# First weights through two kinds of raw tiles, two cache copies placed late, and one buffer pair of decode's keys given to raw weights and evictions

## The chip, the cores and the metric

The program runs on one core of a Trainium2 chip (trn2). The metric is the device time of one execution in microseconds (us). Before the change it was 1180.13 us, the median of 3 runs (1179.48 to 1180.59). Lower is better.

## What is computed

Two layers of a streaming encoder, for a prompt of 1024 tokens and, in the same launch, for 8 sequences that each get 16 new tokens on top of cached keys and values of 1024 tokens. The width is 1024, everything is float32. Cut to what matters:

```python
# layer 0 (A): differential attention + attention to a memory of 256 tokens
q, k, v, gd, mq, gm = a_project(x, w_in_a, cos, sin)          # prompt and samples
od = diff_finish(diff_attend(q, k or cache + k, v or cache + v, mask, lam), g, lam_init)
om = mem_attend(mq, mk, mv)                                   # samples: cached mk, mv
x  = layer_norm(alpha * x + concat(od * silu(gd), om * silu(gm)) @ w_out, ln_g, ln_b)
# layer 1 (B): one shared K/V from x, sliding window of 128 with sinks + memory attention
sks = concat([cache_swa_k, skn], axis=1); svs = concat([cache_swa_v, svn], axis=1)
...                                                           # the same merge
swa_ks, swa_vs = sks[:, -128:], svs[:, -128:]                 # updated rolling buffer
```

The last line is where the two DRAM-to-DRAM copies of this case come from: rows 16 to 127 of the old window caches are an output, copied as they are.

## The kernel before

The tokens are 9 tiles of 128 rows: tiles 0 to 7 are the prompt, tile 8 holds the 128 new tokens. The inputs stand transposed in SBUF as a high and a low part (`th`, `tl`), each weight tile of 128x512 likewise (`wh`, `wl`): float32 is split into two parts, and a product is three products of parts, high by high, high by low and low by high. So each raw tile that is loaded is cast by ScalarE into the high part (line 110) and subtracted from it by VectorE or GpSimd into the low part (line 113). After that the raw tile is free.

Raw tiles come in kinds, with so many buffers each (`RAWS`, line 39): `wraw` for weights, `draw` for decode's cached keys and values and some other inputs of the new tokens, `ev` for what is evicted from the projections' banks on its way to DRAM, and for the x rows of the output projection. The split parts of weights have 8 buffers (`wh`, `wl`), those of decode's raw tiles 4 (`dkh`, `dkl`, function `dk_tiles`). A kind named in `RING` takes its buffers in turn; all `load`s are issued by SyncE (line 119).

`run` puts the weights of all projections into one plan in the order in which they are needed. It first loads the eight weight tiles of the keys and values of heads 0 and 1 (`kvA`, 0; tensor `wA`) with eight calls of `preload(1)`; these subtract on GpSimd and VectorE in turn. Then come `load_x`, which loads each x tile in two halves through buffers called `kh` and `P0` (tile 8 first), and `setup` with small constants. The first projection (`project_kv`) runs the 9 tiles through the eight weights: 24 products of 128x512 a tile, into one of two banks `pj` (line 184). Next is the projection of the queries (`project_q`, weights `wQT`, products of 128x384). Then layer A runs attention of the prompt, decode of the cached sequences (`diff_dec_s` and `diff_dec_v`, whose keys and values go through `raw_split`, `draw` and `dk_tiles`) and the other projections as background. At its end `layer_end` projects the new tokens (`out_first` for tile 8). The two copies `swko` and `swvo` are emitted right after that, in `run`, lines 1407 and 1408.

The order in which instructions are emitted is not the order in which they run. The class `Order` collects all instructions, works out who depends on whom (`depend`: overlapping regions of tiles and tensors, from line 1481), gives each a duration by a table of its own (`cost`), and makes a list schedule over the five engines and the DMA rings (`schedule`), four passes with due times fed back (`due`). An instruction that writes a tile first has to wait there for a free buffer of that kind, and the buffers of a kind are given in the order of emission (`place`). The best of the four orders is then fixed on each engine (`keep`). An instruction that depends on nothing and holds no tile may stand anywhere in it. SyncE runs its issues in that fixed order, one at a time, and waits at an issue whose buffer isn't free.

Of the kernel before, what the change touches and what calls it, by code (L numbers as in the profile page):

```python
# [12 lines left out]
F32R = mybir.dt.float32r  # L13
# [22 lines left out]
HEADS = [1, 2]  # L36
URGENT = 4000
RING = ("wh", "wl", "dkh", "dkl", "draw", "P0", "dP", "ldk")
RAWS = {"wraw": 3, "draw": 4, "ev": 2}
RATES = {('A', 0): (1.0, 3.5, 4), ('A', 1): (0.8, 1.76, 4), ('m', 0): (1.6, 3.25, 7), ('B', 0): (2.17, 2.16, 5), ('B', 1): (0.9, 3.0, 4), ('m', 1): (1.32, 2.18, 5)}  # L40
DECODE = 1.76
DECODE_FIRST = (8, 0, 1, 2, 3, 4, 5, 6, 7)
# [22 lines left out]
class Kernel:  # L65
# [49 lines left out]
    def load(self, tag, src):  # L115
        raw = self.t2([128, 512], tag, bufs=RAWS[tag])[:, :math.prod(src.shape[1:])]
        if len(src.shape) == 3:
# [127 lines left out]
    def setup(self):  # L245
# [14 lines left out]
        nc.gpsimd.memset(self.nhalf, -0.5)  # L260
        lv = self.t2([128, 4, 64], "ev", bufs=RAWS["ev"])
        nc.sync.dma_start(lv, d["lam"].rearrange("o a b -> (o a b)").partition_broadcast(128).rearrange("p (a b) -> p a b", b=64))
        lp = self.t2([128, 2, 64], "ev", bufs=RAWS["ev"])
        nc.vector.tensor_tensor(lp, lv[:, 0::2, :], lv[:, 1::2, :], op=ALU.mult)
# [49 lines left out]
        per = 512 // src.shape[2]  # L314
        self.plan += [(key, src[:, k:k + per, :]) for k in range(0, src.shape[1], per)]

    def preload(self, n, el="dve"):

        for key, src in self.plan[:n]:
            h, lo = (self.take(self.wpool, [128, 512], F32R, x, 8) for x in ("wh", "wl"))  # L320
            c = src.shape[2]
            view = lambda x: x.rearrange("p (a b) -> p a b", b=c)
            self.load_split(view(h), view(lo), "wraw", src, "act", el)
            w = self.loaded.setdefault(key, ([], []))
            for x, y in ((h, w[0]), (lo, w[1])):
                y += [x[:, j * c:(j + 1) * c] for j in range(src.shape[1])]
        del self.plan[:n]
# [310 lines left out]
        self.nc.vector.tensor_tensor_reduce(out, o, x, -1.0, TOP, ALU.add, ALU.min, nm)  # L638

    def dk_tiles(self, n=512):  # L640
        return [self.t2([128, 512], x, F32R, bufs=4)[:, :n] for x in ("dkh", "dkl")]

    def p_tile(self, dt=F32):
        return self.t2([128, 512], "dP", dt, bufs=3)
# [714 lines left out]
    def run(self):  # L1359
        d = self.d  # L1360
        src = {("kvB", 0): d["wKV"]}
        for j in range(4):
            src["gs", j] = d["wBT"][j]
        for l in range(2):
            src["kvA", l], src["gA", l] = d["wA"][l], d["wGA"][l]
            for i in range(2):
                src["M", l, i], src["O", l, i] = d["wM"][l, i], d["wO"][l, i]
            for j in range(4):
                src["q", l, j] = d["wQT"][l, j]
                for i, x in enumerate("qg"):  # L1370
                    src[f"m{x}{l}", j] = (d["wBT"][4:12] if l else d["wAT"])[2 * j + i]
        plan = []
        for l in range(2):
            plan += [("kvB", 0) if l else ("kvA", 0)] + [("q", l, j) for j in range(4)] + ORDER[l] + [("O", l, g) for g in range(2)]
        plan = [(key, src[key]) for key in plan]
        for key, src in plan:
            if key[0] == "M":
                for k in range(0, NK, 2):
                    self.planned(("MT", *key[1:], k), d["memT"][:, k:k + 2, :])
                    self.planned((*key, k), src[:, k:k + 2, :])  # L1380
            else:
                self.planned(key, src)
        for k in range(NK):
            self.preload(1, ("pool", "dve")[k % 2])
        self.load_x()
        self.setup()
        self.background(("kvA", 0), self.layer_a_kv(0))
        self.background(("q", 0), self.project_q(0, (2, 0, 1)))
        for key in ORDER[0]:
            self.background(key, self.filler(*key))  # L1390
        self.finish(("kvA", 0))
        units = [self.diff_dec_units(0), self.diff_dec_units(1), self.mem_dec_units(0)]
        dec = self.side(self.weave(*[[u for g in units for u in g[i]] for i in range(2)]))
        self.layer_a(dec)

        def store(dst, z):
            for c in range(2):
                cols = slice(c * 512, (c + 1) * 512)
                self.nc.sync.dma_start(dst[:, cols], z[:, cols])

        def turn(t, z):
            store(self.x1[t], z)
            self.to_T(t, z[:, 0:512], z[:, 512:1024])

        self.background(("O", 0, 1), self.out_second(0, turn))
        d = self.d
        self.nc.sync.dma_start(d["swko"], d["csk_n"][:, 16:128, :])
        self.nc.sync.dma_start(d["swvo"], d["csv_n"][:, 16:128, :])
        self.background(("kvB", 0), self.layer_b_kv())
        self.finish()  # L1410
        self.background(("q", 1), self.project_q(1, (0, 1, 2)))
        for key in ORDER[1]:
            self.background(key, self.filler(*key))
        self.phase(("B", 0))
        self.credit, self.rate = 0.0, 8.0
        K, V = self.layer_b_build()
        self.need((("q", 1), 0))
        units = [self.swa_dec_units(), self.mem_dec_units(1)]
        dec = self.side(self.weave(*[[u for g in units for u in g[i]] for i in range(2)]))
        self.layer_b(K, V, dec)  # L1420
        self.background(("O", 1, 1), self.out_second(1, lambda t, z: store(d["y"][t], z)))
        self.finish()
# [3 lines left out]
class Order:  # L1426
# [53 lines left out]

    def depend(self):

        self.seen, past = {}, collections.defaultdict(list)
        self.pred, self.uses = [], []
        for i, ins in enumerate(self.ins):
            pred, names = set(), set()
            ops = [(w, self.regions(a)) for w, x in ((0, ins.ins), (1, ins.outs)) for a in x if hasattr(a, "bass_ap")]
            for w, (name, p, m) in ops:
                names.add(name)
                bank = name in self.tiles and self.tiles[name][2]  # L1490
                pred.update(j for j, w2, p2, m2 in past[name] if j != i and p & p2 and m & m2
                            and (w or w2 or bank and self.engine[j] != self.engine[i]))
                past[name].append((i, w, p, m))
            for w, (name, p, m) in ops:
                if w:
                    past[name] = [x for x in past[name] if x[0] == i or x[2] & ~p or x[3] & ~m]
            self.pred.append(pred)
            self.uses.append([x for x in names if x in self.tiles])
        self.succ = [[] for _ in self.ins]
        for i, pred in enumerate(self.pred):  # L1500
            for j in pred:
                self.succ[j].append(i)
# [313 lines left out]
```

## Time and profile before

| | |
|---|---|
| median of 3 runs | 1180.13 us (1179.48 to 1180.59) |
| the profiled execution | 1177.22 us, span 1175.4 us |
| TensorE busy, products | 1120.6 us (95%), 6404 |
| VectorE busy | 823.9 us (70%) |
| ScalarE busy | 731.1 us (62%) |
| GpSimd busy | 355.9 us (30%) |
| moved by DMA | 221.68 MB, mean 189 GB/s |

The span is cut from the first to the last instruction of the program; the profiled execution's own time has a little more around it. TensorE's busy time counts the modelled ends of pipelined products; where products follow each other without a gap, the distance of their starts is their cost. "Idle before" is the time in which an engine did nothing ahead of an instruction, with the instruction or transfer that ended it. PE is TensorE, PEld its weight load, DVE VectorE, ACT ScalarE, POOL GpSimd, SP or SPq SyncE and its issues.

### The profile page before, as it was taken

What the parts mean: (1) busy time and instruction counts of PE and PEld (TensorE: products, weight loads), DVE (VectorE), ACT (ScalarE), POOL (GpSimd) and SP (SyncE); (2) the same over time, 40 slices, a digit from 0 to 9 for tenths busy, and PEclk for the clock granted to TensorE, in tenths of its full rate; (3) what the DMA queues carried; (4) which work ended last, traced back from release to release, by engine and by line L of the source; (5) the groups of instructions that cost most, each with busy time, mean ns of one, the idle gap of its engine ahead of it and who ended that gap; (6) DMA issues with size and microseconds to landing.
All of it is one profiled execution on the core that took longest, in us unless ns stands there. A gap on an engine that the chain in (4) does not pass through costs nothing.

```text
span 1175.4 us, 21494 instructions
## 1 busy us (share of the span) xinstructions
PE 1120.6 (95%) x6404; PEld 991.1 (84%) x6404; DVE 823.9 (70%) x2084; ACT 731.1 (62%) x1863; POOL 355.9 (30%) x570
## 2 busy tenths in 40 slices
PE   4999999999999999999999999999999999999997
PEld 2798898778787887799888888989999999987885
DVE  4333888869999999997774498242667687676277
ACT  5234777757888977987885223243677698687120
POOL 2224334334433322221132044230323232134223
PEclk9999999999999999999999999999999999999999
DMA  8754655766687666786687654554433446667554
GB/s 291 209 153 136 203 155 169 214 170 190 178 254 237 201 178 207 250 269 203 206 264 218 213 186 146 145 161 130 138 120 97 148 123 204 211 208 249 182 176 150
DMA packets 206837, 221.68 MB, mean 189 GB/s; under 512 B 47088, under 2 KB 138224, under 8 KB 206704
## 3 DMA queue, kind: packets, MB, share of 16 engines
q1 hardware_dynamic: 206720, 220.31, 61.9%
q8 instruction: 50, 0.82, 0.3%
q14 instruction: 67, 0.55, 0.2%
HBM read 162.42 MB, written 58.72 MB: 188 GB/s over the span
## 4 chain that ended last, share of the span: by engine, by line
PE 67%; DVE 10%; DMA 9%; ACT 7%; issue 3%; SPq 3%; POOL 1%; DVEq 0%; ACTq 0%; POOLq 0%
PE pj L184 48%; PE tp L126 5%; PE sc L126 4%; PE tp L130 4%; PE do L126 3%; PE dc L126 3%; DVE dkl L113 1%; DMA ldk<-kT_kvA 1%; DVE wl L113 1%; ACT dkh L110 1%; ACT wh L110 1%; DVE m L551 1%; SPq L519 1%; DMA wraw<-wA 1%; ACT ob L726 1%
## 5 line engine op out<-in xcount | busy, mean ns | idle before, releaser
L184 PE MATMUL pj<-wh,th 128*128 128x512 f32 (+1 forms) x648 | 234.6, 364 | 17.6 <-ACT wh L110 10.5
L184 PE MATMUL pj<-wl,th 128*128 128x512 f32 (+1 forms) x648 | 233.5, 362 | 0.3 <-DVE wl L113 0.2
L184 PE MATMUL pj<-th,wh 128*128 128x384 f32 x672 | 230.7, 343 | 2.9 <-ACT ev L374 2.6
L184 PE MATMUL pj<-wh,tl 128*128 128x512 f32 (+1 forms) x648 | 233.0, 361 | 0.0
L184 PE MATMUL pj<-th,wl 128*128 128x384 f32 x672 | 229.4, 341 | 0.0
L184 PE MATMUL pj<-tl,wh 128*128 128x384 f32 x672 | 228.8, 341 | 0.0
L110 ACT CAST wh<-wraw 128x512 fp32r<-128x512 f32 x164 | 101.1, 621 | 90.6 <-PE pj L184 47.6
L184 PEld LDWEIGHTS pj<-wh,th 128*128 128x128 f32 x648 | 122.4, 189 | 38.5 <-ACT wh L110 11.8
L113 DVE TENSOR_TENSOR wl<-wraw,wh 128x512 fp32r<-128x512 f32 x160 | 112.7, 714 | 59.7 <-ACT wh L110 58.8
L113 DVE TENSOR_TENSOR dkl<-draw,dkh 128x512 fp32r<-128x512 f32 (+1 forms) x197 | 136.9, 704 | 23.6 <-ACT dkh L110 22.7
L184 PEld LDWEIGHTS pj<-wl,th 128*128 128x128 f32 x648 | 122.7, 189 | 20.4 <-POOL wl L113 1.2
L113 POOL TENSOR_TENSOR ql<-ldq,qh 128x256 fp32r<-128x256 f32 x96 | 76.6, 801 | 208.7 <-ACT qh L110 153.5
L184 PEld LDWEIGHTS pj<-wh,tl 128*128 128x128 f32 x648 | 122.7, 189 | 18.9 <-issue 0.2
L110 ACT CAST dkh<-draw 128x512 fp32r<-128x512 f32 (+1 forms) x197 | 119.6, 619 | 28.4 <-DMA draw<-dk 6.8
L184 PEld LDWEIGHTS pj<-th,wh 128*128 128x128 f32 x672 | 126.6, 188 | 5.7 <-ACT ev L374 3.4
L184 PEld LDWEIGHTS pj<-tl,wh 128*128 128x128 f32 x672 | 126.6, 188 | 1.5
L184 PEld LDWEIGHTS pj<-th,wl 128*128 128x128 f32 x672 | 126.5, 188 | 1.3 <-issue 0.2
L130 PE MATMUL tp<-ident,P 128*128 128x128 f32 x408 | 68.4, 275 | 3.1 <-DVE sc L550 1.3
L126 PE MATMUL sc<-kh,qh 128*128 128x256 f32 (+2 forms) x224 | 69.2, 316 | 0.3 <-ACT P L559 0.2
L126 PE MATMUL sc<-kh,ql 128*128 128x256 f32 (+2 forms) x224 | 67.3, 311 | 0.0
L559 ACT ACTIVATE P<-sc,m 128x512 f32<-128x512 f32 (+3 forms) x96 | 55.4, 582 | 8.2 <-DVE m L555 4.0
L130 PEld LDWEIGHTS tp<-ident,P 128*128 128x128 f32 x408 | 49.3, 140 | 11.8 <-issue 2.3
(233 smaller groups left out, 2365.8 us busy)
## 6 DMA issues: line engine op xcount, KB each, us to landing
draw<-dk SPq DMA_DIRECT2D x64, 256.0 KB
draw<-dv SPq DMA_DIRECT2D x64, 256.0 KB
ldq<-q SPq DMA_DIRECT2D x128, 64.0 KB
wraw<-wM SPq DMA_DIRECT2D x32, 256.0 KB
wraw<-wO SPq DMA_DIRECT2D x32, 256.0 KB
draw<-cmk SPq DMA_DIRECT2D x32, 256.0 KB
draw<-cmv SPq DMA_DIRECT2D x32, 256.0 KB
wraw<-wBT SPq DMA_DIRECT2D x24, 256.0 KB
```

What stands on the lines that cost most here:

```text
L110: nc.scalar.copy(hi, src)
L113: (nc.vector if el == "dve" else nc.gpsimd).tensor_tensor(lo, src, hi, op=ALU.subtract)
L126: self.last = self.nc.tensor.matmul(*args, **kw).ins.name
L130: self.last = self.nc.tensor.transpose(out, in_, self.ident[:k, :k]).ins.name
L184: ins = self.nc.tensor.matmul(*args, **kw).ins
L519: self.nc.sync.dma_start(dst.rearrange("(j c) t -> c j t", c=32)[:, :, rows], x[rows].rearrange("c (j r) -> c j r", r=32))
L551: nc.vector.tensor_reduce(m2[:, i:i + 1], sc[:, :kn], axis=AX.X, op=ALU.max, negate=True)
L559: nc.scalar.activation(pt[:, 512 * i:512 * i + kn], sc[:, :kn], AF.Exp, bias=nmx, accum_out=st[:, i:i + 1])
L726: nc.scalar.activation(y[at], x[of], AF.Copy, scale=w[of])
```

## The change

Five things. `wraw` gets 4 buffers instead of 3 and `ev` 3 instead of 2 (2 KB a partition each). `dkh` and `dkl` get 3 instead of 4, which frees the same 4 KB. Of the first eight weights every second one is loaded into a `draw` tile instead of a `wraw` tile: those with an even number go to `wraw` and are subtracted on GpSimd, those with an odd number go to `draw` and are subtracted on VectorE (the engines are as before). And in `depend` an instruction that touches no tile at all is made to follow the last TensorE instruction emitted before it; in this kernel that holds for the two copies `swko` and `swvo`. It is a dependence for the schedule alone: it places the copies in SyncE's order and makes no engine wait for another on the chip.

```diff
-RAWS = {"wraw": 3, "draw": 4, "ev": 2}
+RAWS = {"wraw": 4, "draw": 4, "ev": 3}
...
-    def preload(self, n, el="dve"):
+    def preload(self, n, el="dve", tag="wraw"):
...
-            self.load_split(view(h), view(lo), "wraw", src, "act", el)
+            self.load_split(view(h), view(lo), tag, src, "act", el)
...
     def dk_tiles(self, n=512):
-        return [self.t2([128, 512], x, F32R, bufs=4)[:, :n] for x in ("dkh", "dkl")]
+        return [self.t2([128, 512], x, F32R, bufs=3)[:, :n] for x in ("dkh", "dkl")]
...
         for k in range(NK):
-            self.preload(1, ("pool", "dve")[k % 2])
+            self.preload(1, ("pool", "dve")[k % 2], ("wraw", "draw")[k % 2])
...
-        self.pred, self.uses = [], []
+        self.pred, self.uses, product = [], [], None
...
+            uses = [x for x in names if x in self.tiles]
+            if not uses and product is not None:
+                pred.add(product)
+            if self.engine[i] == 0:
+                product = i
             self.pred.append(pred)
-            self.uses.append([x for x in names if x in self.tiles])
+            self.uses.append(uses)
```

## Rows read from the trace of the kernel before

**Rows 1.** The page: busy time, share of the span and instructions of each engine.
```profile
PE 1120.6 (95%) x6404; PEld 991.1 (84%) x6404; DVE 823.9 (70%) x2084; ACT 731.1 (62%) x1863; POOL 355.9 (30%) x570
```

**Rows 2.** 10 us stretches: busy us (instructions) of PE, PEld, DVE, ACT, POOL; clock, DMA share, GB/s.
```profile
0.00:10.00 10.00, 3.42 (x8) 2.70 (x9) 2.94 (x5) 5.73 (x9) 4.13 (x12) 1.00 0.78 265
10.00:20.00 10.00, 8.08 (x29) 4.75 (x28) 7.72 (x16) 7.06 (x13) 1.28 (x1) 1.00 1.06 347
20.00:30.00 10.00, 1.22 (x2) 0.50 (x2) 2.37 (x7) 2.62 (x5) 1.22 (x1) 0.69 0.76 265
30.00:40.00 10.00, 9.89 (x35) 7.90 (x36) 4.74 (x8) 3.38 (x9) 3.31 (x9) 0.80 0.74 232
40.00:50.00 10.00, 10.00 (x45) 8.03 (x44) 2.58 (x5) 3.23 (x8) 2.43 (x8) 1.00 0.75 198
```

**Rows 3.** Timeline of TensorE: start, duration, instructions; in brackets idle before, releaser.
```profile
6.58 0.80 PE L184 MATMUL pj<-wh,th 128*128 128x512 f32 x1 [6.58 <-ACT th L110]
...
7.60 0.63 PE L184 MATMUL pj<-wh,tl 128*128 128x512 f32 x1
8.03 0.63 PE L184 MATMUL pj<-wh,th 128*128 128x512 f32 x1
...
17.95 0.74 PE L184 MATMUL pj<-wh,th 128*128 128x512 f32 x2 [0.91 <-ACT wh L110]
...
28.75 1.22 PE L184 MATMUL pj<-wh,th 128*128 128x512 f32 x2 [8.88 <-ACT wh L110]
...
73.52 0.34 PE L184 MATMUL pj<-th,wh 128*128 128x384 f32 x1
```

**Rows 4.** Timeline of SyncE: start and duration of issues, and what is issued.
```profile
2.12 0.43 SPq L119 DMA_DIRECT2D wraw<-wA  x1
...
6.55 1.62 SPq L119 DMA_DIRECT2D draw<-dk  x2
8.59 0.33 SPq L119 DMA_DIRECT2D wraw<-wA  x1
...
18.12 0.85 SPq L1407 DMA_DIRECT2D swko<-csk_n  x1
...
20.73 0.85 SPq L119 DMA_DIRECT2D wraw<-wA  x2
```

**Rows 5.** Instructions on a tile: duration ns min/median/max, first and last start.
```profile
L113 POOL TENSOR_TENSOR wl<-wraw,wh x4: 1266/1284/1285, 4.5 to 28.8; 128x512 fp32r<-128x512 f32 x4
...
L126 PE MATMUL dc<-dkh,qbd x144: 228/316/501, 104.6 to 1055.7; 128*128 128x512 f32 x64, 128*128 128x256 f32 x64, 128*128 128x144 f32 x16
```

**Rows 6.** The chain of waits in order of time: start, us, what (times).
```profile
20.73 7.33 DMA wraw<-wA
...
648.39 33.76 PE pj L184 x144
```

**Rows 7.** Stretches of 25 us, columns as in rows 2.
```profile
450.00:475.00 25.00, 21.98 (x111) 16.28 (x110) 24.35 (x62) 19.60 (x45) 4.89 (x6) 1.00 0.71 220
...
650.00:675.00 25.00, 25.00 (x109) 20.09 (x108) 10.46 (x16) 6.51 (x11) 2.55 (x2) 1.00 0.66 216
```

**Rows 8.** Waits: who <- whom: us in total, times, longest.
```profile
PE pj L184 <- ACT wh L110: 12.8, 5, 8.9
...
PE pj L184 <- ACT ev L374: 3.1, 2, 2.6
...
ACT dkh L110 <- PE dc L126: 6.0, 10, 1.7
...
ACT dkh L110 <- PE do L126: 2.0, 5, 0.7
...
DVE ev L1314 <- PE pj L184: 30.7, 13, 5.6
```

**Rows 9.** Groups of instructions: busy us, mean ns of one, idle before.
```profile
L113 DVE TENSOR_TENSOR dkl<-draw,dkh 128x512 fp32r<-128x512 f32 (+1 forms) x197 | 136.9, 704 | 23.6 <-ACT dkh L110 22.7
...
L110 ACT CAST wh<-wraw 128x512 fp32r<-128x512 f32 x164 | 101.1, 621 | 90.6 <-PE pj L184 47.6 <-DMA wraw<-wO 12.9 <-DMA wraw<-wA 10.2
```

## The prediction, made before the changed kernel was run

> **What bounds the kernel now.** I read the busy shares first [rows 1]: TensorE is busy for 1120.6 us of a span of 1175.4, so a change gains where TensorE stands still and hardly anywhere else. Then I cut the span into stretches and looked for the standing still. The first 40 us are the worst [rows 2]: 8, 29 and 2 products start in the first three stretches of 10 us, against 45 in a full one. VectorE, ScalarE and GpSimd have idle time there too, so the start waits for data.
>
> What the start owes can be counted. Its work is the first projection (`kvA`, half 0): 9 tiles of 24 products of 128x512. A run of 144 such products elsewhere takes 33.76 us, 0.2344 us each [rows 6], so 216 take 50.6 us. The first one starts at 6.58 us and the next projection's first product (128x384) at 73.52 us [rows 3]. So 73.5 - 6.6 - 50.6 = 16.3 us are lost in between. Three rows say where. The longest wait, 8.88 us, ends with a weight's cast [rows 3]; the chain of waits shows the transfer of that weight, issued at 20.73 us and 7.33 us on its way [rows 6]; SyncE's timeline shows why it went out so late [rows 4]. The first three of the eight weights are issued by 2.12 us, the fourth only at 8.59, the last two at 20.73. There are three `wraw` tiles, so each further weight needs an earlier one split, and GpSimd, which makes every second subtraction, takes 1.28 us for one [rows 5]. In between SyncE issues, in its one order, decode's first keys (`draw<-dk`) and the two DRAM-to-DRAM copies [rows 4] (`swko` and `swvo`, 8 x 112 x 128 floats or 448 KB each). None of that is urgent: the first product on a `dkh` tile starts at 104.6 us [rows 5], and nothing in the kernel reads the copies. From 40 us on TensorE is full again [rows 2]. So the start is bound by the raw tiles of the weights and by SyncE's order.
>
> **The change part by part.** The sum is made against the profiled execution, 1177.22 us with a span of 1175.4; the median of the runs is 1180.13, 2.9 us more, and I carry the difference over to it. About 0.2% of it, 2.4 us, is what a measurement of this kernel can tell from no change.
>
> *First weights.* With four `wraw` tiles and four `draw` tiles all eight weights have a raw tile at time zero, and no issue of them waits for a split. An issue takes SyncE some 0.43 us [rows 4], so eight weights and the four halves of the first two x tiles can be out by about 6 us. They are 12 x 256 KB, 3.1 MB. The first 10 us moved 265 GB/s, 2.65 MB, with next to nothing in the first 2 us; that is about 330 GB/s once it flows [rows 2]. So the last weight is there at about 2.1 + 9.4 = 11.5 us; a cast of 0.62 us and a subtraction of 0.70 on VectorE [rows 9], or 1.28 on GpSimd [rows 5], make it about 13 us. TensorE, with two banks for projections, can work on tiles 8 and 0 meanwhile: 48 products, 11.3 us, from 6.6 us. So the transfers keep about level with it, and TensorE becomes the bound within the second tile. What stays lost: the first products start 0.43 us apart [rows 3], the lower clock level (1.2 GHz); eight of them did in the old trace, 8 x 0.195 = 1.6 us. The second slow stretch (granted clock 0.69 and 0.80 from 20 to 40 us) [rows 2] follows the wait of 8.88 us and should go with it. For weights or x tiles that sit behind another issue I add 2.7 us, three waits like the one of 0.91 us at 17.95 [rows 3]; at best nothing, at worst 6.7, most of one long wait again. That is 4.3 us lost in all: 16.3 - 4.3 = 12.0 us gained, bounds 14.7 and 8.
>
> Two rules speak against this. The Trainium skill, "DMA: Bandwidth & Descriptors", section Specifications, gives about 358 GB/s as what HBM yields to one core. The trace agrees as far as it goes: 10 to 20 us ran at 347 GB/s with the DMA share at 1.06 [rows 2]. By that rule more raw tiles buy nothing while the transfers already run at the limit; as a mechanism of this kernel that is the first rival below.
>
> The Trainium skill, "TensorE: Matmul & The Clock Gate", Part 1, says that the array's clock is throttled by default and that activity releases it. A thinly fed start might by that rule stay at the lower level for all of the 48 products; the sum would then lose 48 x 0.195 = 9.4 us instead of 1.6 and gain about 4, again the first rival's time. The trace speaks against it as far as the granted clock does: 1.00 from 10 to 20 us, though only 29 products ran [rows 2].
>
> *The copies, late.* They now depend on the last product emitted before them, the projection of the new tokens at the end of layer A, so they go out near 650 to 700 us. They take 0.9 MB and two issues, one of them 0.85 us [rows 4], away from the start; that is inside the 12 us. Where they go, TensorE is busy 25.00 of 25.00 us, and the transfers' share is 0.66 [rows 7]. VectorE's evictions there wait for TensorE, 30.7 us over 13 times [rows 8], so their loads come early and cover the copies' few us. I put 0, bounds 0 and +3, the upper one if the copies' 0.9 MB, some 3 us at the rate of the start, come right ahead of a load that is already late.
>
> *`dkh` and `dkl`, four to three.* 197 raw tiles of decode are cast and subtracted, 0.62 + 0.70 us [rows 9], and feed two products or more. With four buffers ScalarE waited 15 times, 8.0 us in all, for a product to free one [rows 8]; the other 182 times one was free. With three I expect this wait about to double. TensorE sees little of it as long as there is background projection to run; but VectorE, which makes the subtractions, is busy 24.35 of 25 us at 450 us [rows 7], so a late start of a pair cannot always be made up. I put +2, bounds -1 and +6; below nothing, because fewer keys held early leave ScalarE and VectorE free for others.
>
> *One more `wraw` and one more `ev` after the start.* TensorE's waits in projections for a cast weight are 12.8 us in 5, of which the start's are 8.9 and 0.9; those behind an eviction of q are 3.1 us in 2 [rows 3, 8]. That bounds the gain at 3.0 + 3.1 = 6.1; one of each could as well come from a full VectorE, so I take -1.5, bounds -3.5 and 0.
>
> The order of all engines is planned anew with these numbers, so small stalls move everywhere; I have no row for that and leave it to the bounds. What is late next at the start are the x tiles and the stores; the steady part of this projection moved 198 GB/s at 40 to 50 us [rows 2], well below what the first stretches moved.
>
> The sum: -12.0 + 0 + 2 - 1.5 = -11.5 us; 1165.7 for an execution like the profiled one and 1168.6 for the median.
>
> **The rivals.** *The first weights come hardly earlier.* Either the transfers are at their limit, so that order alone doesn't help, or the new order on SyncE puts keys that wait for a `draw` tile ahead of x. For it: 347 GB/s at 10 to 20 us [rows 2]. Against it: over a megabyte of what moved then was keys and copies that nobody needed yet. What stays is the copies' 0.9 MB at 0.35 MB per us, 2.6 us, and a little order: some 4 us, 1176.
>
> *The gain is given back in layer A.* There TensorE stands still for up to 3 us in a stretch of 25 while VectorE is nearly full [rows 7]; if the pace from 110 to 650 us is VectorE's and its new order is worse by as much, the time is about 1180. Against it: VectorE's work begins only after the first projections, and shifts with them.
>
> *Slower, by the third `dkh` pair.* A round on the one bank for scores takes two raw tiles. With three pairs only one can be ready ahead, and the next cast waits for the first pair's products; cast and subtraction then take 1.32 us, and the second pair's two products cover 0.47 of it. What else uses the bank covers the rest on idle engines, and not on a full VectorE [rows 7]. If each of 197 tiles costs TensorE 0.1 us, that is 19.7 us instead of my 2: 1168.6 + 17.7 = 1186. It decides from (11.5 + 2) / 197 = 0.07 us a tile. Against it: only 15 waits with four [rows 8].
>
> **How the numbers follow.** Forecast 0.68, own range 1163 to 1175; weights hardly earlier 0.15, at 1176; given back 0.07, at 1180; slower 0.10, at 1186. My terms at their best (-14.7, 0, -1, -3.5) give 1161, at their worst (-8, +3, +6, 0) 1181. A range of 1162 to 1179 holds the forecast, nearly all of the first rival and part of the second. Faster by over 0.2% means under 1177.8: 0.68 + 0.13 = 0.81; within 0.2% 0.09; slower 0.10.
>
> **What would show it.** In the trace of after: all eight issues of `wA` before about 8 us; no TensorE wait of several us before 30 us; the first 128x384 product near 61 to 62 us instead of 73.5; both copies in SyncE's timeline after 640 us, with TensorE full around them. The third pair is harmless if ScalarE's waits of `dkh` for TensorE stay under some 20 us and TensorE's idle time in layer A does not grow. The prediction is wrong if that product comes after 68 us, or if it comes early and the stretches of layer A give it back.

## The result, and the profile after

| | before | after |
|---|---|---|
| median of the runs compared | 1180.36 us (1179.48 to 1181.54, 4 runs) | 1154.88 us (1151.42 to 1155.57, 4 runs) |
| ratio to before, 95% interval | | 0.9778 [0.9756, 0.9800] |
| the profiled execution, span | 1177.22 us, 1175.4 us | 1155.46 us, 1153.7 us |
| TensorE busy | 1120.6 us | 1118.5 us |
| TensorE idle (span less busy) | 54.8 us | 35.2 us |
| first 128x384 product | 73.5 us | 60.4 us |

The change gains 25.5 us. The forecast was a gain of 11.5 us, to 1168.6, in a range of 1162 to 1179; so the direction was right and the size was not.

The page's first section, to be read beside [rows 1]: the work is the same 6404 products.

```profile
PE 1118.5 (97%) x6404; PEld 992.1 (86%) x6404; DVE 821.2 (71%) x2084; ACT 728.9 (63%) x1863; POOL 349.8 (30%) x570
```

The start, in stretches of 10 us (columns as in [rows 2]):

```profile
0.00:10.00 10.00, 4.48 (x8) 2.37 (x9) 2.71 (x3) 5.09 (x8) 4.23 (x13) 1.00 0.76 243
10.00:20.00 10.00, 9.82 (x39) 7.20 (x39) 7.94 (x15) 6.10 (x12) 4.46 (x6) 1.00 0.99 341
20.00:30.00 10.00, 10.00 (x44) 8.05 (x43) 4.43 (x10) 5.03 (x11) 2.88 (x8) 1.00 0.89 263
30.00:40.00 10.00, 10.00 (x44) 7.88 (x43) 3.00 (x6) 2.39 (x5) 1.10 (x4) 1.00 0.87 247
```

TensorE is full from 20 us on; before, only 2 products started between 20 and 30 us [rows 2]. The granted clock reads 1.00 in all four. SyncE's timeline says why, and where the copies went:

```profile
0.73 0.39 SPq L119 DMA_DIRECT2D wraw<-wA  x1
...
1.64 0.43 SPq L119 DMA_DIRECT2D draw<-wA  x1
...
4.97 0.71 SPq L119 DMA_DIRECT2D draw<-wA  x1
...
647.12 2.41 SPq L119 DMA_DIRECT2D wraw<-wO  x4
...
651.62 0.76 SPq L1407 DMA_DIRECT2D swko<-csk_n  x1
...
652.90 0.69 SPq L1408 DMA_DIRECT2D swvo<-csv_n  x1
```

All eight first weights are issued by 5 us; before, the last two went out at 20.73 [rows 4]. The copies stand near 652 us, behind four loads of output weights: with a fourth `wraw` tile four fit. TensorE's timeline shows three waits before 60 us, the first of them for the first x tile (start, duration; in brackets the idle time before and what ended it):

```profile
5.37 0.80 PE L184 MATMUL pj<-wh,th 128*128 128x512 f32 x1 [5.37 <-ACT th L110]
...
7.61 0.80 PE L184 MATMUL pj<-wh,th 128*128 128x512 f32 x1 [0.16 <-ACT wh L110]
...
13.62 0.50 PE L184 MATMUL pj<-wl,th 128*128 128x512 f32 x1 [0.18 <-POOL wl L113]
...
60.40 0.34 PE L184 MATMUL pj<-th,wh 128*128 128x384 f32 x1
```

**Where the gain is.** I cut both spans at the first 128x384 product. Behind it the view counts the same 6189 products in both kernels (a product that runs over the cut counts on both sides), so the two parts can be compared as they are. The stretches of before, then those of after (length, then TensorE's busy time):

```profile
0.00:73.50 73.50, 56.11 (x216) 42.78 (x217) 24.82 (x46) 26.71 (x52) 17.22 (x46) 0.93 0.72 221
73.50:1175.40 1101.90, 1064.47 (x6189) 948.30 (x6187) 799.05 (x2038) 704.35 (x1811) 338.70 (x524) 1.00 0.62 186
```

The same two of after:

```profile
0.00:60.40 60.40, 54.59 (x217) 41.20 (x217) 26.21 (x46) 26.30 (x52) 17.76 (x46) 1.00 0.85 250
60.40:1153.70 1093.30, 1063.89 (x6189) 950.86 (x6187) 794.94 (x2038) 702.56 (x1811) 332.09 (x524) 1.00 0.62 189
```

So 13.1 us come from the start and 8.6 us from the rest, together the 21.7 between the two spans. Of the 13.1, 1.2 us are the first product, which starts at 5.37 us instead of 6.58. The other 3.8 of the 25.5 lie between profiles and medians: the profiled execution of before was quicker than its median (1177.22 against 1180.36), that of after a little slower (1155.46 against 1154.88). In the rest the busy time is the same to 0.6 us; TensorE's idle time there falls from 37.4 to 29.4 us. The waits of projections in the rest show what went (who <- whom: us in total, times, longest). Before:

```profile
PE pj L184 <- ACT ev L374: 3.1, 2, 2.6
PE pj L184 <- ACT wh L110: 2.2, 2, 1.3
PE pj L184 <- DVE wl L113: 0.5, 1, 0.5
PE pj L184 <- DVE ev L445: 0.2, 1, 0.2
```

After:

```profile
PE pj L184 <- ACT ev L374: 0.4, 2, 0.2
PE pj L184 <- ACT wh L110: 0.3, 1, 0.3
```

That is 6.0 us before and 0.7 after. The remaining 2.7 us of idle time went from waits in attention, some of which became shorter and some longer. This is one planned order of each kernel; the last part of the experiments shows others.

### The profile page after: what moved, and what is told of

The parts are those of the page before. It is cut to its first block, busy times and chain, and to the rows that moved or that the text cites. A ratio compares the mean times of both kernels' runs of the same rounds, so it can differ in the third digit from the quotient of the medians.

```text
span 1153.7 us, 21451 instructions
## 1 busy us (share of the span) xinstructions
PE 1118.5 (97%) x6404; PEld 992.1 (86%) x6404; DVE 821.2 (71%) x2084; ACT 728.9 (63%) x1863; POOL 349.8 (30%) x570
## 4 chain that ended last, share of the span: by engine, by line
PE 71%; DVE 9%; DMA 8%; ACT 5%; issue 4%; SPq 1%; POOL 1%; DVEq 0%; ACTq 0%; POOLq 0%
PE pj L184 50%; PE tp L126 5%; PE sc L126 4%; PE do L126 4%; PE tp L130 4%; PE dc L126 3%; DVE dkl L113 2%; DVE wl L113 1%; DMA draw<-dk 1%; ACT ob L726 1%; DMA ldk<-kT_kvA 1%; DVE m L551 1%; DMA wraw<-wO 1%; PE dc L130 1%; DVE dP L638 1%
## 5 line engine op out<-in xcount | busy, mean ns | idle before, releaser
L113 POOL TENSOR_TENSOR ql<-ldq,qh 128x256 fp32r<-128x256 f32 x96 | 74.2, 777 | 248.8 <-ACT qh L110 195.3
L110 ACT CAST wh<-wraw 128x512 fp32r<-128x512 f32 x160 | 98.6, 622 | 62.7 <-PE pj L184 40.7
L113 DVE TENSOR_TENSOR wl<-wraw,wh 128x512 fp32r<-128x512 f32 x156 | 109.8, 715 | 33.3 <-ACT wh L110 33.1
```

The source lines that it names most:

```text
L110: nc.scalar.copy(hi, src)
L113: (nc.vector if el == "dve" else nc.gpsimd).tensor_tensor(lo, src, hi, op=ALU.subtract)
```

## The experiments

Each run is told by its median, its ratio to the kernel before on the same chip, and two lengths of its profile: the start (up to the first 128x384 product) and the rest (the other 6189 products). For the rest, the waits of projections for a cast weight (`wh`, line 110) and for an eviction of q (`ev`, line 374) stand beside it, us in total. A rest comes from one profiled execution.

| kernel | median | ratio [95%] | start | rest | `wh` | `ev` |
|---|---|---|---|---|---|---|
| before | | | 73.5 | 1101.9 | 2.2 | 3.1 |
| `s_weights` | 1170.42 | 0.9914 [0.9889, 0.9938] | 64.2 | 1103.3 | 1.6 | 4.1 |
| `s_copies` | 1182.50 | 1.0001 [0.9979, 1.0022] | 69.5 | 1110.6 | 4.9 | 2.3 |
| `s_start` | 1175.73 | 0.9950 [0.9926, 0.9973] | 59.9 | 1115.3 | 4.4 | 6.6 |
| `s_bufs` | 1159.79 | 0.9824 [0.9797, 0.9851] | 62.2 | 1095.2 | none | 2.1 |
| `b_dk3` | 1180.79 | 1.0005 [0.9986, 1.0024] | 74.9 | 1104.4 | 2.0 | 2.5 |
| `b_wraw4` | 1171.55 | 0.9935 [0.9912, 0.9958] | 67.7 | 1101.5 | 0.4 | 4.0 |
| `b_ev3` | 1172.76 | 0.9930 [0.9911, 0.9950] | 74.9 | 1099.7 | 1.4 | none |
| `a_wraw3` | 1166.03 | 0.9867 [0.9823, 0.9910] | 59.6 | 1108.5 | 4.5 | 1.5 |
| `a_ev2` | 1165.85 | 0.9867 [0.9830, 0.9904] | 62.6 | 1102.0 | 0.4 | 4.9 |
| `a_w5` | 1154.89 | 0.9771 [0.9730, 0.9812] | 61.3 | 1088.2 | none | none |
| after | 1154.88 | 0.9778 [0.9756, 0.9800] | 60.4 | 1093.3 | 0.3 | 0.4 |

### The start and the buffers, apart

**Weights through both kinds and the copies late, buffers as before** (`s_start`), from the changed kernel:

```diff
-RAWS = {"wraw": 4, "draw": 4, "ev": 3}
+RAWS = {"wraw": 3, "draw": 4, "ev": 2}
...
-        return [self.t2([128, 512], x, F32R, bufs=3)[:, :n] for x in ("dkh", "dkl")]
+        return [self.t2([128, 512], x, F32R, bufs=4)[:, :n] for x in ("dkh", "dkl")]
```

> The two changes at the start alone: every second first weight through a draw tile and the copies late; wraw 3, ev 2 and four dkh pairs as before. The whole change moved the first query product from 73.5 to 60.4 us and ended 21.8 us earlier in the profiles, so some 9 us came after the start. Theory 1 (the start gives its 13 us, the rest comes from the buffers): about 1167 us, first query product near 60 us, and the stretches of layer A and B as before. Theory 2 (the new order of all engines brought the rest by chance): anything from 1150 to 1172, with gains or losses spread over the layers. Theory 3 (the start itself pays more than 13 us, since what follows is bound by its end): about 1155.

Measured: 1175.73 us, outside all three theories. The start is even shorter than after's, 59.9 us, 13.6 less than before; but the rest is 13.4 us longer than before's, so the profile's span is the old one (1175.2). This edit alone is the case "given back". The place that shows it best is the output projection of layer A, where TensorE was full before [rows 7]. TensorE's timeline there:

```profile
668.49 0.39 PE L184 MATMUL pj<-wh,tl 128*128 128x512 f32 x1
671.70 0.74 PE L184 MATMUL pj<-wh,th 128*128 128x512 f32 x2 [2.82 <-ACT wh L110]
...
673.65 0.63 PE L184 MATMUL pj<-wh,tl 128*128 128x512 f32 x1
674.07 0.63 PE L184 MATMUL pj<-wl,th 128*128 128x512 f32 x1
```

The chain of waits through that stop (start, us, what):

```profile
663.01 7.94 DMA wraw<-wO
```

SyncE's timeline leads up to that transfer:

```profile
657.00 1.73 SPq L119 DMA_DIRECT2D wraw<-wO  x3
658.78 0.77 SPq L1407 DMA_DIRECT2D swko<-csk_n  x1
659.60 1.39 SPq L1408 DMA_DIRECT2D swvo<-csv_n  x1
...
663.01 1.20 SPq L119 DMA_DIRECT2D wraw<-wO  x2
```

Three output weights go out, then the copies, then the next weight, which is 7.94 us on its way behind them. In before the same load is issued at 668.23 us with no copies ahead of it, and its cast starts at 672.94, 4.7 us later. The wait is paid twice: soon after it, from 673.24 to 676.63 us, eight products start 0.43 us apart instead of 0.23, the lower clock level. That holds for the whole rest. Its busy time for the same 6189 products is 1073.48 us against 1064.47 before, and between 50 and 1150 us the granted clock is below 1.00 in seven stretches of 25 us, against one in the profile of before. The clock that is missing in them, 25 us times what lacks to 1.00, adds up to 10.2 us against 1.8, which is nearly all of the 9.0 us (columns as in [rows 2]):

```profile
59.90:1175.20 1115.30, 1073.48 (x6189) 954.12 (x6187) 799.27 (x2038) 702.79 (x1811) 339.10 (x524) 0.99 0.62 186
...
450.00:475.00 25.00, 22.86 (x105) 17.57 (x104) 22.67 (x65) 19.19 (x49) 4.05 (x5) 0.86 0.68 214
...
650.00:675.00 25.00, 22.18 (x91) 17.13 (x91) 9.37 (x14) 4.97 (x8) 0.00 (x0) 0.96 0.63 208
675.00:700.00 25.00, 25.00 (x123) 20.55 (x122) 23.69 (x46) 7.72 (x13) 11.21 (x10) 0.97 0.54 181
```

**Buffers alone** (`s_bufs`): four `wraw`, three `ev`, three `dkh` and `dkl`; first weights through `wraw` alone and the copies early.

```diff
-            self.preload(1, ("pool", "dve")[k % 2], ("wraw", "draw")[k % 2])
+            self.preload(1, ("pool", "dve")[k % 2])
...
-                pred.add(product)
+                pass
```

> The buffers alone: wraw 4, ev 3, three dkh pairs; the first weights all through wraw, the copies anywhere. Theory 1: 1168 to 1171, with the start only a little better (one more wraw tile) and some 9 us gained after it. Theory 2: anything within 8 us of before. My prediction's own terms (+2 for the pairs, -1.5 for the buffers) would give 1178 to 1181 plus whatever the fourth wraw tile does at the start.

Measured: 1159.79 us, 1.76% [1.49, 2.03] less than before, the largest part of the whole (2.22%) and more than any theory held. Two things follow. The buffers gain in the rest (6.7 us by the profile). And they shorten the start nearly as much as the rerouted weights do, to 62.2 us, with both copies still issued at 20.38 and 21.73 us: with a fourth `wraw` tile four weights are issued at once and the others by 13.9 us, in time for the second tile.

**Weights alone** (`s_weights`): the rerouted weights, with buffers and copies as before (the first diff of this section and the second line of the last).

> Every second first weight through a draw tile, nothing else: the copies stay free to be placed anywhere, buffers as before. If the raw tiles were what bound the start, it gains nearly as much as both start changes together: first query product near 61 us, about 1168. If the copies had a large part, the last weights still land late: first query product at 65 to 70 us, about 1173.

Measured: 1170.42 us, start 64.2, rest 1103.3 (before 1101.9), between the two forecasts. The 9.3 us of the start stay. What it lacks against after's start is partly x tiles that come late (TensorE waits 1.34 us at 44.26 and 0.61 at 29.88 for their cast) and an eviction (0.53 us at 33.74).

**Copies alone** (`s_copies`): only the dependence of the copies, everything else as before.

> The copies late, nothing else. SyncE saves two issues of 0.85 and 0.70 us before the last two weights, and 0.9 MB leave the start. If the raw tiles bind, the gain is some 2 to 4 us: first query product at 70 to 72 us, 1176 to 1178. If the copies were the larger part, the first query product comes at 65 us, about 1172.

Measured: 1182.50 us, no difference to before, though both forecasts held a gain. Its start is 4.0 us shorter, and the rest 8.7 longer, with the same stop in the output projection (2.65 us, at 678.28). So the copies' late place isn't free: with three `wraw` tiles it costs what it gains.

### One buffer at a time

From the kernel before:

```diff
 # b_dk3: the line of dk_tiles alone; b_wraw4 and b_ev3 have it too
-        return [self.t2([128, 512], x, F32R, bufs=4)[:, :n] for x in ("dkh", "dkl")]
+        return [self.t2([128, 512], x, F32R, bufs=3)[:, :n] for x in ("dkh", "dkl")]
...
-RAWS = {"wraw": 3, "draw": 4, "ev": 2}
+RAWS = {"wraw": 4, "draw": 4, "ev": 2}     # b_wraw4
+RAWS = {"wraw": 3, "draw": 4, "ev": 3}     # b_ev3
```

> The kernel before with three dkh pairs and nothing else (4 KB a partition stay unused). The two start changes alone ended only 0.5% earlier, though their first query product came 13.6 us earlier; the buffers alone ended 1.8% earlier. So the prediction's terms for the buffers are wrong, and this takes the loss apart. My prediction's step: +2 us (-1 to +6), ScalarE's waits of dkh for TensorE about twice 8.0 us: 1181 to 1184. If the third pair is free: within 1 us of before. If fewer pairs held early even help, as in the lower bound: 1176 to 1180.

Measured: 1180.79 us, ratio 1.0005 [0.9986, 1.0024]. The third pair costs between -1.7 and +2.8 us, so my +2 isn't excluded, nothing at all fits as well, and the bound of +6 and the 19.7 of the slower rival are excluded.

> The kernel before with three dkh pairs and a fourth wraw tile. Theory 1 (the raw weight tile is what paid: at the start, and at each change of weights later): first query product near 62 us as with both buffers, 1161 to 1166. Theory 2 (the ev tile paid): first query product near 65 us or later, 1170 to 1176. Theory 3 (chance of the new order): no relation between the start and the end.

Measured: 1171.55 us with a start of 67.7, by its numbers theory 2. The stop of 8.9 us at the start is gone; but a new one ends at 38 us, with an eviction. TensorE's timeline:

```profile
33.41 0.39 PE L184 MATMUL pj<-wh,tl 128*128 128x512 f32 x1
38.12 0.80 PE L184 MATMUL pj<-wh,th 128*128 128x512 f32 x1 [4.33 <-ACT ev L484]
38.72 0.63 PE L184 MATMUL pj<-wl,th 128*128 128x512 f32 x1
```

and ScalarE's ahead of it:

```profile
35.09 0.62 ACT L110 CAST th<-kh 128x512 fp32r<-128x512 f32 x1 [3.82 <-DMA kh<-xT]
36.37 0.62 ACT L110 CAST th<-P 128x512 fp32r<-128x512 f32 x1 [0.66 <-DMA P<-xT]
37.42 0.37 ACT L471 COPY ev<-pj 128x256 f32<-128x256 f32 x1 [0.44 <-DMA kd<-ev]
37.69 0.38 ACT L484 COPY ev<-pj 128x256 f32<-128x256 f32 x1
```

The bank is free when ScalarE has evicted it. ScalarE waits 0.44 us for the store `kd<-ev` of an earlier eviction, that is for one of two `ev` tiles; but before that its planned order has it cast x tiles that come late, and the eviction stands behind them. So the buffer alone doesn't make up these 4.33 us. In `s_bufs`, which differs from this kernel by the third `ev` alone, an eviction stands ahead of those casts, at 28.78 us, and the longest wait for `ev` at line 484 in the first 60 us is 0.27 us. It is likely, and not shown, that the planner put it behind them because two tiles were too few.

> The kernel before with three dkh pairs and a third ev tile. Theory 1: the start as before (first query product 70 to 74 us), about 1176 to 1179, a little from evictions. Theory 2 (the ev tile paid): 1168 to 1172 with the gain in the layers, at an unchanged start.

Measured: 1172.76 us, and a start of 74.9: without a fourth `wraw` the third `ev` does nothing there. That is theory 2. Its gain is in the rest, and the waits for `ev` of line 374 are gone from it. (Its profile is of the slowest of ten executions, 3.9 us above their median, so the rest of 1099.7 shows too little of the gain.) At the start the third `ev` shortens nothing by itself (74.9, as in `b_dk3`), but 5.5 us once there are four `wraw` (67.7 to 62.2): the second buffer shows only when the first is no longer missing.

### The change with one buffer taken back

> The changed kernel with three wraw tiles instead of four (three ev, three dkh pairs, first weights through draw, copies late). Singly added to the kernel before, the fourth wraw tile was worth 0.65% and the third ev tile 0.7%, together 1.8%; the copies placed late held TensorE up by some 4 us near 670 us where wraw had three tiles, since the next output weights then waited behind the copies. Theory 1 (the wraw tile pays in the layers and covers the late copies): the stop near 660 us comes back, and the time is 6 to 10 us above the change, 1161 to 1165. Theory 2 (the start's eight raw tiles are all that wraw gives here, and draw covers them): within 2 us of the change save for the stop, 1157 to 1159.

```diff
-RAWS = {"wraw": 4, "draw": 4, "ev": 3}
+RAWS = {"wraw": 3, "draw": 4, "ev": 3}     # a_wraw3
+RAWS = {"wraw": 4, "draw": 4, "ev": 2}     # a_ev2
```

Measured: 1166.03 us, 1 us above theory 1. The start stays (59.6); the stop in the output projection is back:

```profile
669.28 0.39 PE L184 MATMUL pj<-wh,tl 128*128 128x512 f32 x1
672.50 0.74 PE L184 MATMUL pj<-wh,th 128*128 128x512 f32 x2 [2.83 <-ACT wh L110]
```

The stop goes with the two conditions together. Of all 20 kernels of this case, TensorE stands still for more than 0.4 us between 640 and 690 us in three only, `s_start`, `s_copies` and `a_wraw3`: those with late copies and three `wraw`. Early copies with three `wraw` don't show it, nor late ones with four, in any of the five planned orders below.

With the earlier runs this gives the price of the late copies by the length of the rest (the last three of the five comparisons also differ in the kind of tile of the first weights). With three `wraw`: +8.7 (`s_copies` against before), +12.0 (`s_start` against `s_weights`), +8.8 (`a_wraw3` against `b_ev3`). With four: -1.9 (after against `s_bufs`), +0.5 (`a_ev2` against `b_wraw4`). By the medians the price with three is some 5 to 10 us. The visible stop is 2.7 to 2.8 us of it; much of the rest is clock: `s_copies` has 1071.6 us of busy time there, 7.1 more than before for the same products. How much of that is the copies' and how much the new order's is open: the kernel before has 1064.5 to 1071.5 in the five orders below.

> The changed kernel with two ev tiles instead of three. Theory 1 (the ev tile pays by itself): 1161 to 1165, with TensorE's losses spread over the stretches where projections are evicted (75 to 650 us and the change from layer A to B near 750 us), none near 660 us. Theory 2 (no part of its own): within 2 us of the change, 1153 to 1157.

Measured: 1165.85 us, 1 us above theory 1. TensorE is full around the copies, so the fourth `wraw` alone covers them. What is missing is, in part, what `ev` covers: 4.9 us of waits for `ev` of line 374 (after 0.4) and 2.2 us of the start. `a_wraw3` and `a_ev2` are one order each, and the changed kernel itself reaches 1165.25 in another order (below); the stop and the waits are what they show, not the size of the 11 us.

**Further along the same line** (`a_w5`): a second pair of `dkh` and `dkl` gone, for a fifth `wraw` and a fourth `ev`.

```diff
-RAWS = {"wraw": 4, "draw": 4, "ev": 3}
+RAWS = {"wraw": 5, "draw": 4, "ev": 4}
...
-        return [self.t2([128, 512], x, F32R, bufs=3)[:, :n] for x in ("dkh", "dkl")]
+        return [self.t2([128, 512], x, F32R, bufs=2)[:, :n] for x in ("dkh", "dkl")]
```

> The changed kernel one step further: five wraw, four ev, two dkh pairs. Dropping the fourth pair alone cost nothing. If a third pair is spare as well and raw tiles go on paying: 1145 to 1153. If decode needs two pairs in use and one ahead: ScalarE's waits of dkh for TensorE several times as long as with three pairs, TensorE's idle time in layer A up, 1160 to 1190.

Measured: 1154.89 us, the same as after within some 5 us, and neither forecast. Decode runs as well with two pairs: ScalarE's waits for a product to free one are 10.5 us in all. The waits for `wh` and for `ev` of line 374 are gone, but they were only 0.7 us, so little was left to gain with more raw tiles.

### How much is the planner's order

All engines' orders are planned anew whenever a number changes. To see how far that alone moves the time, I changed a number in the planner's table that changes nothing of the work, its guess of the time in ns from a transfer's issue to its landing: `LANDING`, 2200 in both kernels, to 2000, 2100, 2300 and 2400, in the kernel before (`b_land`, `b_l21`, `b_l23`, `b_l24`) and in the changed one (`a_land`, `a_l21`, `a_l23`, `a_l24`).

```diff
-    LANDING, RATE, ISSUE, WAKE = 2200.0, 17.0, 460.0, 45.0
+    LANDING, RATE, ISSUE, WAKE = 2000.0, 17.0, 460.0, 45.0
```

> The kernel before, planned with a transfer's landing of 2000 ns in place of 2200 in the planner's own table; nothing that the chip has to do is changed. It shows how far a new order alone moves the time. If the order is robust: within 2 us of before, so differences of 4 us and more between the kernels of this study need a cause. If chance is large: up to 8 us either way, and differences of that size between kernels prove little.

> The changed kernel, planned with a landing of 2000 ns in the planner's table in place of 2200, as was done with the kernel before (0.35% slower there). If the gain of the layers belongs to the buffers: within 0.4% of the change, 1150 to 1160. If it was a lucky order: 1160 to 1168, where the sum of the start's 13 us and nothing else would lie.

> The kernel before planned with a landing of 2100 ns. By theory 1 it lies within 4 us of 1180; by theory 2 it may lie anywhere from 1172 to 1188, first query product near 73 us.

> The changed kernel planned with a landing of 2100 ns; the first of three pairs (2100, 2300 and 2400 ns, beside 2000 and 2200 that have run) of the changed kernel and the kernel before under the same number in the planner's table. Theory 1 (the gain beyond the start is the buffers'): the pairs differ by 22 to 28 us each, the changed kernel at 1152 to 1158 in most. Theory 2 (it is the order's chance, the change itself is worth the start's 12 to 13 us and a few more): the changed kernel lies at 1158 to 1170, and the mean of the pairs' differences is 13 to 20 us. First query product at 60 to 62 us by both.

> The kernel before planned with a landing of 2300 ns: 1176 to 1187, 18 to 27 us above the changed one; about 13 us above it if the buffers' part was chance.

> The changed kernel planned with a landing of 2300 ns, the fifth pair. Four pairs differ by 18 to 27 us, and the stretches give 12 us at the start, some 5 at the end of layer A with four wraw tiles, some 6 in layer B with three ev tiles. By these sums it lies at 1153 to 1162; with the start alone it would lie at 1165 to 1170.

> The kernel before planned with a landing of 2400 ns. Theory 1: within 4 us of 1180. Theory 2: 1172 to 1188.

> The changed kernel planned with a landing of 2400 ns. Theory 1: 1152 to 1158. Theory 2: 1158 to 1170 with the start as early as in the others, and the difference to them in the layers.

| `LANDING` | before: median | ratio [95%] | start, rest | changed: median | ratio [95%] | start, rest | medians' difference |
|---|---|---|---|---|---|---|---|
| 2000 | 1183.59 | 1.0035 [1.0017, 1.0054] | 72.1, 1109.5 | 1165.25 | 0.9859 [0.9820, 0.9898] | 60.6, 1102.3 | 18.3 |
| 2100 | 1178.15 | 0.9991 [0.9973, 1.0009] | 72.3, 1103.0 | 1158.03 | 0.9818 [0.9782, 0.9855] | 60.3, 1096.6 | 20.1 |
| 2200 | 1180.36 | | 73.5, 1101.9 | 1154.88 | 0.9778 [0.9756, 0.9800] | 60.4, 1093.3 | 25.5 |
| 2300 | 1183.49 | 1.0034 [1.0019, 1.0050] | 73.3, 1107.0 | 1156.09 | 0.9813 [0.9782, 0.9844] | 60.4, 1093.8 | 27.4 |
| 2400 | 1185.55 | 1.0037 [1.0016, 1.0059] | 73.0, 1111.2 | 1158.54 | 0.9815 [0.9783, 0.9847] | 61.5, 1091.2 | 27.0 |

The order alone moves the kernel before by 7.4 us and the changed one by 10.4. The change itself is worth 18 to 27 us, 23.7 in the mean (the pair at 2000 ran on two chips; by the ratios it is 20.8): by the profiles' means 12.2 in the start (72.8 to 60.6) and 11.1 in the rest (1106.5 to 1095.4). So the gain over the forecast isn't one order's luck; the 25.5 are about 2 us above the mean. Neither theory of `a_l21` came out whole: two of the five pairs lie under its 22 to 28 us, and the mean lies above the 13 to 20 of chance. `a_land` by itself fell where a lucky order had been expected (1160 to 1168), which only the other pairs correct.

The waits of projections in the rest, us, by order (`ev` of line 374, `wh`, and all that the list names):

| `LANDING` | before: `ev`, `wh`, all | changed: `ev`, `wh`, all |
|---|---|---|
| 2000 | 4.8, none, 5.6 | 0.5, none, 5.5 |
| 2100 | 4.6, 0.2, 7.2 | 0.4, 0.9, 2.8 |
| 2200 | 3.1, 2.2, 6.0 | 0.4, 0.3, 0.7 |
| 2300 | 2.4, 3.2, 6.0 | 0.2, 2.1, 4.6 |
| 2400 | 5.2, 1.6, 10.0 | none, none, 4.8 |

The waits for `ev` go in every order. Those for `wh` don't, and the fall from 6.0 to 0.7 is the best of the five; the mean is 7.0 to 3.7. The 11.1 us of the rest are 7.1 of idle time (38.2 to 31.1), less than half of it these waits, and 4.0 of busy time for the same products (1068.3 to 1064.3).

## Why the prediction was right and wrong, point by point

**The start: right.** Forecast -12.0, measured -13.1 in the pair of profiles and -12.2 over five orders. The causes were those named: weights without a raw tile, SyncE's order, and the slow clock behind the long wait. The bounds (-14.7 and -8) held. Of the 16.3 us lost between the first product and the next projection 4.4 are left, where I forecast 4.3; that is luck in the parts, since the first ten products cost 3.0 us by their slower pace, not 1.6, the waits after the first product are 0.3 us, not 2.7, and some 1.1 us lie in single wider steps between products. The transfers were no limit that mattered: 341 GB/s from 10 to 20 us, about what it was [rows 2], with 39 products instead of 29, because the eight weights had gone out before, in the first 5.7 us; decode's keys and the next projection's weights, four loads each, were still issued in those 10 us. The Trainium skill, "DMA: Bandwidth & Descriptors", section Specifications, has about 358 GB/s for one core. No stretch of 10 us shown here is above it, single microseconds are (403 GB/s from 11 to 12 us), and it did not decide. That refutes the first rival. Its clock variant falls with it: from 10.64 us on products started 0.23 us apart for the most part, though TensorE was not yet full; only the first ten were 0.42 us or more apart, about the eight that I had counted. (The granted clock reads 1.00 in every 10 us stretch to 40 us, in the first one too, where the pace is that of the lower level; so the pace, and not that column, is what I go by.) So the thin feeding that the rule in the Trainium skill, "TensorE: Matmul & The Clock Gate", Part 1, made me weigh did not keep the lower level. One thing I had wrong: I took the eight raw tiles at time zero and the copies' new place for the cause of the gain. `s_bufs` has 11.3 of the 13.1 us without either, from one more `wraw` and one more `ev`. The two ways overlap, and their gains must not be added.

**The copies: right in size, by an argument that wasn't sufficient.** I put 0, because TensorE is full there and loads come early. `s_copies` and `a_wraw3` refute that as a reason: with three `wraw` TensorE is as full, and the late copies cost some 5 to 10 us, above my upper bound of 3. In the changed kernel they cost nothing because the fourth `wraw` lets four output weights go out ahead of them. The cover for one edit was another edit of the same change. That my 0 held is luck.

**The third `dkh` pair: right in sign at most.** Forecast +2, measured -1.7 to +2.8. ScalarE's waits for a product to free a pair went from 8.0 us [rows 8] to 9.4, where I expected about twice as much (ScalarE's waits after):

```profile
ACT dkh L110 <- PE dc L126: 8.4, 14, 2.0
...
ACT dkh L110 <- PE do L126: 1.0, 2, 0.7
```

The slower rival is refuted, and `a_w5` refutes it for two pairs as well.

**One more `wraw` and `ev` after the start: the mis-sized term.** I put -1.5, bounds -3.5 and 0, out of 6.1 us of waits that I had named, since "one of each could as well come from a full VectorE". (Of the 6.1, 0.7 us lay in the start, at 13.39 us, so the rest held 5.3.) The step that failed is this cut of the list, to a quarter in the forecast and to about half in the bound. For `ev` the list did name its buffer: in all kernels here with three or more `ev` the waits of line 374 are at most 2.1 us, in all with two 2.3 to 6.6. For `wh` it did so less surely: none to 4.9 us with three `wraw`, none to 2.1 with four or five. By the medians, less the difference of the starts, the third `ev` is worth some 8 us in the rest (`b_ev3` against `b_dk3`) and the fourth `wraw` some 2 (`b_wraw4` against `b_dk3`), each in one order: some -10 where I put -1.5, and more than the list held. The cut had no row behind it, and even the whole list was too little, since idle time in attention and the busy time fell too.

**The steps together.** For the rest I forecast 0 + 2 - 1.5 = +0.5; the pair of profiles shows -8.6, five orders in the mean -11.1. Of the 9.1 us between forecast and pair, 3.8 are named waits of the mis-sized term (-5.3 instead of -1.5), up to 2 the third pair, and the remaining 3 or so waits in attention that no term of mine held. Over the five orders the named waits give less, 3.3 us, and other idle time 3.8 and shorter busy time 4.0; no term held the last two. I wrote that I leave the new order "to the bounds", but the bounds of the rest reached only from -4.5 to +9, summed from the terms; nothing in them stood for an order that moves the time by 7 to 10 us. The last part of the miss is the step from profile to median: I carried the 2.9 us over as a constant, and before stands 3.1 above its profile and after 0.6 below. The difference goes with the granted clock: 0.984 to 0.993 in the timed runs of before, 0.996 to 0.997 in those of after. The profiled execution of before had 0.992 where its timed runs have 0.989 in the mean; at the 0.9 us for each 0.001 by which time and clock go together in them, that is, as an estimate, 2.6 of the 3.1 us. Fewer waits leave fewer stretches at the lower level: that this is why after's clock is higher is argued, not shown.

**"Given back" as a rival: right as an outcome, for another kernel and another reason.** `s_start` is that case: 13.6 us gained at the start and 13.4 lost. I had blamed VectorE's pace; the rows show waits for `wh` and `ev` (11.0 us in the rest against 5.3 before) and the lower clock after them.

**What stays open.** In which waits of attention the other idle time went, and how much of it is order: single profiles differ by more than that. How the gain of the rest divides between the third `ev`, the fourth `wraw` and the clock is not settled either: each was taken singly in one order only, and orders alone move the time by 7 to 10 us. The third `ev` is worth 8.2 us by the median (`b_ev3`, interval 5.9 to 10.5 us) while the waits that it removes are 3.1 us.

## What to carry to other kernels

When one edit frees a place, look at what else stands in the same issue order behind that place: a transfer that nobody reads is only free where the loads behind it have buffers to be issued ahead of it. Do not halve a wait that a list names for a buffer's user without a row that says why: with one more `ev` nearly all of its waits were gone in five orders out of five, and where it was added alone the time fell by more than they were. For `wraw` the list changed with the order, so read it in more than one. And where a second buffer limits right behind the first, the two have to be tried together: at the start here the fourth `wraw` alone gained 7 us, the third `ev` alone nothing, and both together 13. Where a planner orders everything anew, measure both kernels in a few neutral orders before believing, or bounding, a few microseconds.

## What the runs showed of the hardware that I had not expected

A wait of a few microseconds costs more than its length: soon after the stop of 2.82 us that ends at 671.70 in `s_start` eight products start 0.43 us apart, against 0.23 before it, and in that kernel's rest the same 6189 products are busy 9.0 us longer than before, with 8.5 us more of missing clock. The same shows as scatter: 83 timed runs of before, on five chips, lie between 1174.7 and 1186.6 us with the granted clock between 0.984 and 0.993, and within a chip the longer runs tend to be those with the lower clock (correlation -0.70 about each chip's means, some 0.9 us for each 0.001).
